# Down stage, second block: two more groups by seven, with sums of weights formed on the spot, in another order

## The chip, the cores and the metric

The kernel runs on one core of one Trainium2 chip. The metric is device time in microseconds (us). The kernel before was run three times: 1461.22, 1462.11 and 1462.31 us, median 1462.11.

## What is computed

The reference is one layer of a hybrid of attention and feed-forward over 256 tokens of width 2048, all in 32-bit floats. The change touches its last line alone, the product with `w_down`:

```python
h2 = rms_norm(x, g_ffn[l])
u = causal_depthwise_conv(h2 @ w_up[l], conv_w[l], conv_b[l])
u_gate, u_val = jnp.split(u, 2, axis=-1)
x = x + (jax.nn.silu(u_gate) * u_val) @ w_down[l]      # (256 x 5632) @ (5632 x 2048)
```

## The kernel before

**Precision.** Every 32-bit operand is split in a high part `hi` (a cast on ScalarE, ACT) and a remainder `lo` (a subtraction on VectorE, DVE). A product is three matmuls on TensorE (PE): hi by hi, lo by hi, hi by lo (function `three`, lines 326 to 330). Line 328 is the first, 329 the second, 330 the third, which is the first to read the weights' lo. `parts` (line 318) makes hi (line 322) and lo (line 323) of a piece of weights of up to 1024 columns. There are four buffers for hi and four for lo.

**Blocks and groups.** The Down stage computes its output in two blocks of 1024 columns (`nb` 0 and 1). In each, the 44 k-tiles of 128 rows are taken in 22 groups of two. A group is a 2 x 2 by 2 x 2 block product: two token tiles (t) by two k-tiles (j), times two k-tiles by two column halves (n).

- By **eight** (`eight`, line 389): the eight products, accumulated in four PSUM banks X. That is 24 matmuls, two loads of 512 KB (line 384) and two pieces to split.
- By **seven** (`seven`, line 412): Strassen's scheme in Winograd's form with seven products, 21 matmuls, accumulated in the same X and in four further banks Y. It needs four sums of weights, T1, T3, T4 and T2, and four sums of activations, FS1 to FS4. The sums of weights were formed earlier in the kernel in the background and written to DRAM (`pair_sums_ahead`, `half_sums`, `kept_for`). `seven` loads half a k-tile together with T3 into `raw0` (lines 415, 416), the other k-tile into `raw1` (384), T1 and T2 (419), and T4 (421): five DMAs and 1.75 MiB, and splits them as three pieces of 1024 columns and one of 512.
- In the gate stage the sums of weights are formed on the spot: `prepared` (line 436) loads both k-tiles a group ahead and makes the four sums by four additions on DVE (lines 440 to 443) into two buffers of their own; `seven_here` uses them.

**Sums of activations.** A "form" (`form`, line 1276, by `pair_sums`, line 332) makes FS1 to FS4 of a group on DVE (337 to 342) and splits them (344 on ACT, 346 on DVE). Eleven are made in block 0 and reused by block 1; those for groups 11 and above are written over activations that block 1's eights have read (`s_of`, line 1261). All forms share one scratch buffer, tag `ts` (`tmp_d`, line 1274), with the gathering below.

**The order.** A string gives each block's order: `e` is an eight, `s` a seven, `f` a form. The strings are `d_plans`, lines 228 to 231. Groups by seven count up from 0, eights from the number of sevens. The code is traced in that order, and Tile's scheduler makes each engine's instruction order from it; in this stage PE's order isn't pinned by the code.

**Buffers of raw weights.** Loads are counted from the start of the stage. After the first ten, the count modulo six picks the place (`raw_tile`, line 1109): four share the four buffers of tag `raw`, one has a buffer of the stage (`raw_d`, line 1291), one has `xu`. Every load of weights goes through SyncE's queue (SP), in order.

**The end.** After the last seven, `gather` (line 348) adds the Y banks to the result in eight additions on DVE (lines 355 to 365), in a chain through two scratch halves. It advances at `tick`, twice a group. In the block's very last group (`by_bank`, line 390) the products are ordered bank by bank; the last bank is cut in two, its second half called `apart`. Lines 1303 and 1307 add the X banks to the result and lines 1305 to 1310 store it through ACT's queue.

Of the kernel before, what the change touches and what calls it, by code (L numbers as in the profile page):

```python
# [12 lines left out]
ALU = mybir.AluOpType  # L13
# [4 lines left out]
NT = S // P  # L18
# [24 lines left out]
def hybrid_block(  # L43
# [25 lines left out]
    nc = tc.nc  # L69
# [12 lines left out]
    def bank(name):  # L82
        return pp.tile([P, 512], F32, tag="bank", name=name)
# [14 lines left out]
    def later(gen):  # L98
        waiting.append(gen)
# [3 lines left out]
    def tick(beside=True):  # L103
        if beside:
            for g in background:
                next(g, None)
        while waiting and len(active) < window[0]:
            active.append([waiting.popleft(), 0])
        for a in list(active):
            if a[1] > 0:  # L110
                a[1] -= 1
                continue
            try:
                a[1] = next(a[0]) or 0
            except StopIteration:
                active.remove(a)
# [7 lines left out]
    def finish():  # L124
        while waiting or active:
            tick(beside=False)
# [76 lines left out]
    def k_tiles(name):  # L203
# [23 lines left out]
    g_plans = (("", "esesesee", "esesesee"), ("esesesee", "esesesee", "esesesee"))  # L227
    d_plans = (
        "efefefef" + "sef" * 4 + "ssefsfssfssee",
        "efefef" + "sss" + "esss" * 3 + "ssee",  # L230
    )
    T1, T3, T4, T2 = range(4)
    FS2, FS4, FS3, FS1 = range(4)
    in_order = tc.keep_in_program_order
# [5 lines left out]
        (name, by_k(w), nb, pr, h)  # L240
        for name, w, plans in (("o", w_out, o_plans), ("d", w_down, d_plans))
        for nb, plan in enumerate(plans)
        for pr in range(plan.count("s"))
        for h in range(2)
    )

# [71 lines left out]
    def parts(src, name):  # L318
        n = src.shape[1]
        hi = wp.tile([P, PIECE], F32R, tag="hi", bufs=SBUFS, name=f"hi_{name}")  # L320
        lo = wp.tile([P, PIECE], F32R, tag="lo", bufs=SBUFS, name=f"lo_{name}")
        nc.scalar.copy(hi[:, :n], src)  # L322
        nc.vector.tensor_tensor(lo[:, :n], src, hi[:, :n].bitcast(F32), ALU.subtract)  # L323
        return [(hi[:, i : i + 512], lo[:, i : i + 512]) for i in range(0, n, 512)]

    def three(o, ah, al, w, first=False, last=False):
        fix = in_order if ordered[0] else lambda ins: ins
        fix(nc.tensor.matmul(o, lhsT=ah, rhs=w[0], start=first, stop=False))  # L328
        fix(nc.tensor.matmul(o, lhsT=al, rhs=w[0], start=False, stop=False))  # L329
        fix(nc.tensor.matmul(o, lhsT=ah, rhs=w[1], start=False, stop=last))  # L330
# [36 lines left out]
    def blocked(name, w, nb, n0, plan, pair, sums, raw_tile, t4_tile, gathered, ready=None, form=None, apart=None):  # L367

        wv = by_k(w)
        X = [[bank(f"x{name}{nb}_{t}_{n}") for n in range(2)] for t in range(NT)]  # L370
        Y = []
        ns = plan.count("s")

        def a_of(p, j, t):
            v = pair(p, j)
# [6 lines left out]
        def load(k):  # L382
            raw = raw_tile(f"raw_{name}{nb}_{k}")
            nc.sync.dma_start(raw, wv[:, k, n0 : n0 + PIECE])
            return raw

        go_on = lambda: tick(beside=name != "g")
# [48 lines left out]
        def prepared(p):  # L436
            raw0, raw1 = load(2 * p), load(2 * p + 1)
            t13, t42 = (t4_tile(f"t{i}_{name}{nb}_{p}") for i in range(2))
            b0, b1, u, v = (w.rearrange("p (n c) -> p n c", n=2) for w in (raw0, raw1, t13, t42))
            nc.vector.tensor_tensor(u[:, 0], b0[:, 0], b0[:, 1], ALU.add)  # L440
            nc.vector.tensor_tensor(u[:, 1], b0[:, 1], b1[:, 1], ALU.add)
            nc.vector.tensor_tensor(v[:, 1], u[:, 0], b1[:, 1], ALU.add)
            nc.vector.tensor_tensor(v[:, 0], v[:, 1], b1[:, 0], ALU.add)
            return raw0, raw1, t13, t42
# [14 lines left out]
            three(Y[1], *f_of(p, FS2), T2w, first, last)  # L459
            go_on()  # L460

        by_seven = seven_here if name == "g" else seven
        ahead = {}
        s, e = 0, ns
        for i, c in enumerate(plan):
            if c == "s":
                if s == 0:
                    if ready:
                        ready()
                    Y += [bank(f"y{name}{nb}_{j}") for j in range(4)]  # L470
                by_seven(s, s == 0, s == ns - 1)
                s += 1
                if s == ns:
                    later(gathered(n0, Y))
            elif c == "f":
                form()
            else:
                eight(e, i == 0, i == len(plan) - 1)
                e += 1
            if name == "g" and plan[i + 1 : i + 2] == "s":  # L480
                ahead[s] = prepared(s)
        finish()
        return X

# [200 lines left out]
    w = {}  # L685
# [30 lines left out]
    for k in range(KT):  # L716
# [18 lines left out]
        for _ in range(0 if k < 3 else 1 if k < 8 else 3):  # L735
            if squares:
                j, t = squares.popleft()
# [273 lines left out]
    for m in range(2):  # L1011
        gate = []
        for b, plan in enumerate(g_plans[m]):
            g, bias = [], []
# [26 lines left out]
            def ready():  # L1041
                finish()
                if "heads" not in issued:
                    issued.add("heads")
                    window[0] = 2
                    later(sigmoids(gate[0] + gate[1]))
                biases()
# [7 lines left out]
            if not plan:  # L1055
# [6 lines left out]
            X = blocked(  # L1062
                "g", w_in, f"{m}{b}", c0, plan, lambda p, j: xT(2 * p + j), lambda p, f: xs[:, p, f], raw_g, block,
                gathered, ready,
            )
# [5 lines left out]
        for n in range(2):  # L1071
            acc = gate[branches[0][3]][n]
            for i, (w, k0, nk, b) in enumerate(branches):
# [5 lines left out]
                for t in range(NT):  # L1079
                    g = gate[b][n]  # L1080
# [40 lines left out]
    for nb, plan in enumerate(o_plans):  # L1121
        X = blocked(
            "o", w_out, nb, nb * PIECE, plan, lambda p, j: mT[p][:, j], lambda p, f: ms[p][:, f], raw_o, t4_o[nb],
            lambda n0, Y: gather(n0, Y, block),
        )
# [20 lines left out]
    def a_pair(p):  # L1146
        if p < FA // 2:
            return aT[:, 2 * p : 2 * p + 2]
        if not ends:
            ends.append(ends_tile("a_ends", F32R).rearrange("p i (k c) -> p i k c", k=2))  # L1150
        return ends[0][:, p - FA // 2]
# [64 lines left out]
    for f0 in range(0, FT, 4):  # L1216
# [5 lines left out]
        for s in range(2):  # L1222
            ps = [bank(f"u{f0 + i}_{s}") for i in range(4)]
            c0 = s * D_FF + f0 * P
            for k in range(0, KT, 2):
                hi, lo = piece(upv[:, k : k + 2, c0 : c0 + 512], 2, 512, f"u{f0}_{s}_{k}")
                for j in range(2):
                    first, last = k + j == 0, k + j == KT - 1
                    for i in range(4):
                        c = slice(i * P, (i + 1) * P)  # L1230
# [20 lines left out]
        return dn[0].tile(shape, dt, tag=tag, name=name)  # L1251

    ov = out[0].rearrange("(t p) d -> p t d", p=P)
    N0, N1 = (plan.count("s") for plan in d_plans)
    sf = xt_pool.tile([P, 28, 2, P], F32R, tag="xt", name="sf")
    sf_more, sf_rest = [], []
    assert N0 == 11
    a_blocks = aT.rearrange("p k (l t q) -> p k l t q", l=2, t=NT)
    formed = [0]

    def s_of(p, f):


        if f == FS1:
            return a_blocks[:, 2 * p, :, 1]
        if p < 9:
            return sf[:, 3 * p + f]
        if p == 9:
            return sf_more[0][:, f] if f < 2 else sf_rest[2]
        if p == 10:  # L1270
            return sf[:, 27] if f == 0 else sf_rest[f - 1]
        return a_blocks[:, 2 * (p - N0 + N1) + f // 2, :, f % 2]

    tmp_d = lambda name: place([P, PIECE], F32, "ts", name)

# [17 lines left out]
    for nb, plan in enumerate(d_plans):  # L1293
        apart = [] if nb == 1 else None
        X = blocked(
            "d", w_down, nb, nb * PIECE, plan, lambda p, j: a_pair(p)[:, j], s_of, raw_d, junk,
            lambda n0, Y: gather(n0, Y, tmp_d), None, form, apart,
        )
        for t in range(NT):
            for n in range(2):  # L1300
                c = nb * PIECE + n * 512
                o = xres[:, t, c : c + 512]
                nc.vector.tensor_tensor(o, o, X[t][n], ALU.add)
                if (nb, t, n) == (1, 1, 1):
                    nc.scalar.dma_start(ov[:, t, c : c + 256], o[:, :256])
                    c, o = c + 256, o[:, 256:]
# [35 lines left out]
```

## Time and profile before

| | us |
|---|---|
| median of three runs | 1462.11 |
| the profiled execution's own time | 1461.49 |
| its span, first to last instruction | 1459.8 |
| Up stage's last matmul and Down stage's first | 1233 |
| first product of block 1 | 1345.2 |
| last matmul | 1455.8 |

The profile is of one execution. Each engine's instructions have a start and a duration; "L323" is line 323 of the kernel; PEld is the loading of a matmul's stationary operand, beside PE. Names are those of the program's tiles with numbers left out: `hi_d` and `lo_d` are split weights that were loaded from `w_down` (or half from there and half T3), `hi_t_d` split sums, `xd` and `yd` the banks X and Y, `sf` and `aT` sums of activations and activations, `fw` a form's scratch, `raw_g`, `t_g` and `xg` the gate stage's likes. `SPq` and `ACTq` are instructions that issue a DMA. In rows of single instructions the first number is the start and the second the duration; a row with "x2" holds two in a run. In rows of groups the numbers behind the bar are the busy time in us and the mean duration in ns.

### The profile page before, as it was taken

The numbers are of one execution on the slowest core, as the hardware profiler recorded it, in microseconds if no ns is written. First come the engines' busy times: TensorE is split into PE (matmuls) and PEld (weight loads), VectorE is DVE, ScalarE is ACT, GpSimd is POOL, SyncE is SP. The second block draws the span as 40 slices with busy tenths as digits, with TensorE's granted clock in tenths as the row PEclk, the third lists the DMA queues.
The fourth block names the chain that finished last, engine by engine and source line by source line (L and its number), as shares of the span: only waits on it lengthen the run. The fifth ranks groups of instructions, "written<-read, shape, count | busy, mean of one in ns | idle before, by whom it ended". The sixth has DMA issues, their size and how long they took to land.

```text
span 1459.8 us, 20547 instructions
## 1 busy us (share of the span) xinstructions
PE 1454.0 (100%) x7314; PEld 1230.1 (84%) x7314; DVE 1213.4 (83%) x1791; ACT 850.0 (58%) x1212; POOL 19.3 (1%) x48
## 2 busy tenths in 40 slices
PE   9999999999999999999999999999999999999998
PEld 7888888888888888888888888888888888888887
DVE  5778777776898899997887888888888877999878
ACT  6755454564564555545666556556556565676665
POOL 0000000010000000000000000000000000000000
PEclk9999999999999999999999999999999999999999
DMA  9697798777668576788877888888888866899995
GB/s 312 202 330 248 267 341 288 238 241 222 209 207 269 172 231 198 270 265 263 276 196 232 288 266 306 278 273 299 283 281 298 267 200 202 253 291 333 299 324 222
DMA packets 162534, 381.08 MB, mean 261 GB/s; under 512 B 12234, under 2 KB 27486, under 8 KB 158334
## 3 DMA queue, kind: packets, MB, share of 16 engines
q1 hardware_dynamic: 161022, 377.52, 78.9%
q10 hardware_dynamic: 1328, 2.11, 0.4%
q8 instruction: 57, 0.93, 0.3%
q14 instruction: 47, 0.39, 0.1%
q0 software_dynamic: 80, 0.13, 0.0%
HBM read 343.01 MB, written 36.70 MB: 260 GB/s over the span
## 4 chain that ended last, share of the span: by engine, by line
PE 97%; DVE 1%; DMA 1%; issue 0%; SPq 0%; ACT 0%; DVEq 0%; ACTq 0%
PE u L1231 22%; PE u L1232 11%; PE xd L329 3%; PE xd L330 3%; PE xd L328 3%; PE xg L330 3%; PE xg L329 3%; PE xg L328 3%; PE s L328 2%; PE s L330 2%; PE f L330 2%; PE f L328 2%; PE f L329 2%; PE s L329 2%; PE b L330 2%; PE b L328 2%
## 5 line engine op out<-in xcount | busy, mean ns | idle before, releaser
L1231 PE MATMUL u<-hT,hi_u 128*128 128x512 f32 x1232 | 428.3, 394 | 0.0
L1232 PE MATMUL u<-hT,lo_u 128*128 128x256 f32 x1232 | 341.3, 277 | 0.0
L1231 PEld LDWEIGHTS u<-hT,hi_u 128*128 128x128 f32 x1232 | 231.0, 188 | 53.8
L143 DVE TENSOR_TENSOR lo_u<-raw_u,hi_u 128x1024 fp32r<-128x1024 f32 x176 | 215.1, 1222 | 73.2 <-ACT hi_u L142 71.9
L142 ACT CAST hi_u<-raw_u 128x1024 fp32r<-128x1024 f32 x176 | 184.7, 1050 | 135.0 <-PE u L1231 106.7
L1232 PEld LDWEIGHTS u<-hT,lo_u 128*128 128x128 f32 x1232 | 231.2, 188 | 0.0
L323 DVE TENSOR_TENSOR lo_d<-raw_d,hi_d 128x1024 fp32r<-128x1024 f32 x88 | 106.7, 1222 | 16.2 <-ACT hi_d L322 13.8
L322 ACT CAST hi_d<-raw_d 128x1024 fp32r<-128x1024 f32 x88 | 91.7, 1053 | 38.8 <-PE xd L329 17.8
L322 ACT CAST hi_g<-raw_g 128x1024 fp32r<-128x1024 f32 (+1 forms) x80 | 77.1, 972 | 48.9 <-PE xg L329 19.2
L323 DVE TENSOR_TENSOR lo_g<-raw_g,hi_g 128x1024 fp32r<-128x1024 f32 (+1 forms) x80 | 88.6, 1119 | 4.1 <-ACT hi_g L322 4.1
L142 ACT CAST hi_f<-raw_f 128x1024 fp32r<-128x1024 f32 (+1 forms) x40 | 38.5, 967 | 51.8 <-PE f L329 42.8
L330 PE MATMUL xg<-lo_g,xT 128*128 128x512 f32 x175 | 68.1, 389 | 0.0
L329 PE MATMUL xg<-hi_g,xT 128*128 128x512 f32 x175 | 68.1, 389 | 0.0
L328 PE MATMUL xg<-hi_g,xT 128*128 128x512 f32 x175 | 68.1, 389 | 0.0
L143 DVE TENSOR_TENSOR lo_f<-raw_f,hi_f 128x1024 fp32r<-128x1024 f32 (+1 forms) x40 | 44.6, 1118 | 22.3 <-ACT hi_f L142 21.7
L143 DVE TENSOR_TENSOR lo_s<-raw_s,hi_s 128x1024 fp32r<-128x1024 f32 (+1 forms) x40 | 44.7, 1117 | 20.9 <-ACT hi_s L142 20.9
L1231 PE MATMUL u<-hT_rest,hi_u 128*128 128x512 f32 x176 | 62.0, 394 | 0.0
L142 ACT CAST hi_b<-raw_b 128x1024 fp32r<-128x1024 f32 x32 | 33.6, 1051 | 45.2 <-DMA raw_b<-in_w_br_fox_dram 15.8
L142 ACT CAST hi_s<-raw_s 128x1024 fp32r<-128x1024 f32 (+1 forms) x40 | 38.4, 961 | 36.8 <-PE s L329 23.9
L1182 ACT ACTIVATE y<-u,taps 128x256 f32<-128x256 f32 x88 | 49.6, 596 | 16.3 <-DVE u L1177 16.2
L330 PE MATMUL xd<-lo_d,aT 128*128 128x512 f32 x148 | 57.6, 389 | 0.0
L328 PE MATMUL xd<-hi_d,aT 128*128 128x512 f32 x148 | 57.6, 389 | 0.0
(520 smaller groups left out, 3473.1 us busy)
## 6 DMA issues: line engine op xcount, KB each, us to landing
raw_u<-in_w_up_dram SPq DMA_DIRECT2D x176, 512.0 KB, 4.5
raw_g<-in_w_in_dram SPq DMA_DIRECT2D x96, 512.0 KB, 4.4
raw_d<-in_w_down_dram SPq DMA_DIRECT2D x63, 512.0 KB, 5.4
pre_d<-in_w_down_dram SPq DMA_DIRECT2D x17, 1024.0 KB, 6.2
kept_d<-pre_d SPq DMA_DIRECT2D x17, 1024.0 KB, 6.2
raw_f<-in_w_in_dram SPq DMA_DIRECT2D x32, 512.0 KB, 4.9
raw_s<-in_w_in_dram SPq DMA_DIRECT2D x32, 512.0 KB, 5.2
raw_t_d<-kept_d SPq DMA_DIRECT2D x25, 512.0 KB, 5.8
```

The costliest lines, as they stand in the source:

```text
L142: pin(nc.scalar.copy(hi[:, :m], raw[:, :m]))
L143: pin(nc.vector.tensor_tensor(lo[:, :m], raw[:, :m], hi[:, :m].bitcast(F32), ALU.subtract))
L322: nc.scalar.copy(hi[:, :n], src)
L323: nc.vector.tensor_tensor(lo[:, :n], src, hi[:, :n].bitcast(F32), ALU.subtract)
L328: fix(nc.tensor.matmul(o, lhsT=ah, rhs=w[0], start=first, stop=False))
L329: fix(nc.tensor.matmul(o, lhsT=al, rhs=w[0], start=False, stop=False))
L330: fix(nc.tensor.matmul(o, lhsT=ah, rhs=w[1], start=False, stop=last))
L1182: nc.scalar.activation(y, u[:, 2:], AF.Identity, scale=tap(2), bias=tap(3))
L1231: nc.tensor.matmul(ps[i], lhsT=hi[:, j, c], rhs=hT(k + j), start=first, stop=False)
L1232: nc.tensor.matmul(ps[i][:, :S], lhsT=lo[:, j, c], rhs=hT(k + j)[:, :S], start=False, stop=last)
```

## The change

The second block's plan becomes `efss` four times, then `issefssisse`. Sixteen groups go by seven and six by eight, in place of fourteen and eight; five forms in place of three. `i` is a new kind of group by seven. Its weight sums are formed on the spot: `begun`, traced right behind the group ahead, loads both k-tiles and makes T1, T3 and T2 by three additions, T1 and T3 into a scratch buffer of tag `ts`, T2 over half of the first k-tile's own buffer. `seven_over` splits the other half, forms T4 over it, and goes on as `seven_here` does. The groups that have their sums in DRAM are still fourteen in this block, with other numbers.

```diff
     d_plans = (
         "efefefef" + "sef" * 4 + "ssefsfssfssee",
-        "efefef" + "sss" + "esss" * 3 + "ssee",
+        "efss" * 4 + "issefssisse",
     )
+    sevens = lambda plan: [c for c in plan if c in "si"]
...
-        for pr in range(plan.count("s"))
+        for pr, c in enumerate(sevens(plan))
+        if c == "s"
...
+        def begun(p):
+            raw0, raw1, t13 = load(2 * p), load(2 * p + 1), tmp_d(f"t_{name}{nb}_{2 * p}")
+            b0, b1, u = (w.rearrange("p (n c) -> p n c", n=2) for w in (raw0, raw1, t13))
+            nc.vector.tensor_tensor(u[:, 0], b0[:, 0], b0[:, 1], ALU.add)
+            nc.vector.tensor_tensor(u[:, 1], b0[:, 1], b1[:, 1], ALU.add)
+            nc.vector.tensor_tensor(b0[:, 1], u[:, 0], b1[:, 1], ALU.add)
+            return raw0, raw1, t13
+
+        def seven_over(p, first, last):
+            raw0, raw1, t13 = ahead.pop(p)
+            (B00,) = parts(raw0[:, :512], f"{name}{nb}_{2 * p}")
+            three(Y[0], *a_of(p, 0, 0), B00, first, last)
+            nc.vector.tensor_tensor(raw0[:, :512], raw0[:, 512:], raw1[:, :512], ALU.add)
+            B10, B11 = parts(raw1, f"{name}{nb}_{2 * p + 1}")
+            three(X[0][0], *a_of(p, 1, 0), B10)
+            three(X[0][1], *f_of(p, FS4), B11)
+            go_on()
+            T1w, T3w = parts(t13, f"t_{name}{nb}_{2 * p}")
+            three(Y[2], *f_of(p, FS1), T1w, first, last)
+            three(Y[3], *f_of(p, FS3), T3w, first, last)
+            T4w, T2w = parts(raw0, f"t_{name}{nb}_{2 * p + 1}")
+            three(X[1][0], *a_of(p, 1, 1), T4w)
+            three(Y[1], *f_of(p, FS2), T2w, first, last)
+            go_on()
...
+            elif plan[i + 1 : i + 2] == "i":
+                ahead[s] = begun(s)
...
-        return a_blocks[:, 2 * (p - N0 + N1) + f // 2, :, f % 2]
+        over = a_pair(p - N0 + N1).rearrange("p k (l t q) -> p k l t q", l=2, t=NT)
+        return over[:, f // 2, :, f % 2]
```

The rest of the diff replaces counts of `s` by counts of `s` and `i`, and picks the function by the letter.

More of the change, by code (lines that the diff above doesn't have):

```diff
@@ L371, in blocked @@
         Y = []
-        ns = plan.count("s")
+        ns = len(sevens(plan))
         def a_of(p, j, t):
@@ L460, in seven_here @@
             go_on()
-        by_seven = seven_here if name == "g" else seven
+        def begun(p):
[21 more added lines that the diff above has]
+            go_on()
+        by_seven = {"s": seven_here if name == "g" else seven, "i": seven_over}
         ahead = {}
@@ L465, in blocked @@
         for i, c in enumerate(plan):
-            if c == "s":
+            if c in "si":
                 if s == 0:
@@ L470, in blocked @@
                     Y += [bank(f"y{name}{nb}_{j}") for j in range(4)]
-                by_seven(s, s == 0, s == ns - 1)
+                by_seven[c](s, s == 0, s == ns - 1)
                 s += 1
@@ L1253, in hybrid_block @@
     ov = out[0].rearrange("(t p) d -> p t d", p=P)
-    N0, N1 = (plan.count("s") for plan in d_plans)
+    N0, N1 = (len(sevens(plan)) for plan in d_plans)
     sf = xt_pool.tile([P, 28, 2, P], F32R, tag="xt", name="sf")
```

## The prediction

> **What bounds the kernel now.** I read the totals first, then the Down stage by engine, then single instructions there.
>
> ```profile
> span 1459.8 us, 20547 instructions
> PE 1454.0 (100%) x7314; PEld 1230.1 (84%) x7314; DVE 1213.4 (83%) x1791; ACT 850.0 (58%) x1212; POOL 19.3 (1%) x48
> ```
>
> PE is busy for the whole span, but ends of matmuls are modelled, so the second block (from 1345.2 us to its last matmul) has to be read from distances between starts:
>
> ```profile
> 1345.20:1455.80 110.60, 110.60 (x494) 91.66 (x492) 92.49 (x109) 68.45 (x82) 0.00 (x0) 1.00 0.84 287
> 1375.80:1395.50 19.70, 19.70 (x88) 16.31 (x87) 15.27 (x15) 13.14 (x15) 0.00 (x0) 1.00 0.95 332
> ...
> 1366.49 0.39 PE L328 MATMUL yd<-hi_d,aT 128*128 128x512 f32 x1
> 1366.94 0.39 PE L330 MATMUL yd<-lo_d,aT 128*128 128x512 f32 x1
> 1371.25 0.39 PE L328 MATMUL yd<-hi_d,aT 128*128 128x512 f32 x1
> ```
>
> In the windows the columns after the length are PE, PEld, DVE, ACT, POOL, clock, DMA share, GB/s. A group by seven has 21 matmuls: 1371.25 - 1366.49 = 4.76 us, or 0.2267 us each. An eight has 24, 5.44 us. One eight and three sevens are 87 matmuls, 19.72 us, the length of the second window. The block's 486 products would take 110.2 us, and its window is 110.6. PE waits for nothing here at full clock, so the matmul count sets the block's length.
>
> How much the others may slip, the casts and subtractions tell (ACT, then DVE; the number before "<-" in brackets is idle time):
>
> ```profile
> 1363.10 1.05 ACT L322 CAST hi_d<-raw_d 128x1024 fp32r<-128x1024 f32 x1 [0.74 <-PE yd L329]
> 1367.82 1.06 ACT L322 CAST hi_d<-raw_d 128x1024 fp32r<-128x1024 f32 x1 [0.47 <-PE yd L329]
> 1364.19 2.59 DVE L323 TENSOR_TENSOR lo_d<-raw_d,hi_d 128x1024 fp32r<-128x1024 f32 x2 [1.10 <-ACT hi_d L322]
> 1366.87 1.83 DVE L323 TENSOR_TENSOR lo_t_d<-raw_t_d,hi_t_d 128x1024 fp32r<-128x1024 f32 x2
> 1368.91 2.58 DVE L323 TENSOR_TENSOR lo_d<-raw_d,hi_d 128x1024 fp32r<-128x1024 f32 x2 [0.21 <-ACT hi_d L322]
> 1347.10 1.21 DVE L323 TENSOR_TENSOR lo_d<-raw_d,hi_d 128x1024 fp32r<-128x1024 f32 x1
> 1348.23 0.41 DVE L340 TENSOR_TENSOR fw<-fw 128x256 f32<-128x256 f32 x1
> ```
>
> Casts are released by PE, which frees one of four hi buffers. The first lo of the group at 1366.49 ends at 1364.19 + 1.23 = 1365.42 and is first read at 1366.94. So the lead is 1.5 us, however early the weights come. A 1024-wide subtraction occupies DVE for 1348.23 - 1347.10 = 1.13 us when the next operation doesn't depend on it, though its record is 1.22 long.
>
> **The change, part by part.** *Matmuls.* Two eights become groups by seven: 6 fewer, 6 x 0.2267 = -1.36 us. That is all there is to gain.
>
> *DMAs.* Counting issues, block two had 8 x 2 + 14 x 5 = 86, and has 6 x 2 + 14 x 5 + 2 x 2 = 86. Bytes: 8 x 1 + 14 x 1.75 = 32.5 MiB, and 6 + 24.5 + 2 = 32.5 again. The densest pattern gets lighter: one eight and three sevens moved 332 GB/s without a PE gap; one eight and two sevens are 4.5 MiB in 14.96 us, or 315 GB/s. I cost the transfers at nothing, hidden behind PE; without that cover, see the third rival.
>
> *Activation sums.* Two forms more. Their DVE and ACT work, of which three lay in the window already:
>
> ```profile
> L337 DVE TENSOR_TENSOR fw<-aT 128x512 f32<-128x512 f32 x3 | 2.1, 687 | 0.0
> L340 DVE TENSOR_TENSOR fw<-fw 128x256 f32<-128x256 f32 x3 | 1.2, 417 | 0.0
> L341 DVE SCALAR_TENSOR_TENSOR fw<-fw 128x128 f32<-128x128 f32 x3 | 0.9, 292 | 0.1
> L342 DVE TENSOR_TENSOR fw<-fw 128x128 f32<-128x128 f32 x3 | 0.9, 288 | 0.0
> L344 ACT CAST aT<-fw 128x128 fp32r<-128x128 f32 x12 | 3.1, 296 | 1.3 <-DVE fw L342 0.7 <-DVE fw L340 0.5
> L346 DVE TENSOR_TENSOR aT<-fw,aT 128x128 fp32r<-128x128 f32 x12 | 2.7, 286 | 0.0
> ```
>
> One form is 0.69 + 0.42 + 0.29 + 0.29 + 4 x 0.29 = 2.8 us of DVE by durations, some 2.2 by distances (each 0.08 less where nothing depends). A stretch "efss" then needs 2 x 1.13 + 2.2 + 2 x (3 x 1.13 + 0.61) = 12.5 us of DVE in 14.96 of PE. It fits: nothing on the path. Their writes overlay activations that the eight just ahead reads, as before; three such stood without a gap.
>
> *The two groups with sums formed on the spot.* Each adds four 512-wide additions, at 0.61 (an independent one) to 0.72 us (a dependent one, below): 2.45 us at the lower price. Against an eight, it also has 1.5 pieces more to split. DVE then needs 4.0 + 2.45 = 6.4 us in a group of 4.76. Three additions are issued ahead, in the preceding seven's slot: 4.0 + 1.83 = 5.83 against 4.76, 1.07 late; the fourth stays in its own, 4.61 against 4.76. The lead is thinner here too: the new group's first piece has only 3 matmuls, so its second and third piece have 12 matmuls of cover instead of 15, that is 0.68 us less, 1.5 - 0.7 = 0.8. So 1.07 - 0.8, about 0.3 us of PE stall per group, if the weights have landed. Next late are casts and lo of the following seven, which recovers 0.76 a group. Whether they have landed, only the gate stage's like groups show (waits of its first addition, one such row, and the only PE gap among its 15):
>
> ```profile
>   DMA raw_g<-in_w_in_dram: 11.5, 9
> 378.44 0.69 DVE L440 TENSOR_TENSOR t_g<-raw_g 128x512 f32<-128x512 f32 x1 [2.25 <-DMA raw_g<-in_w_in_dram]
> 421.76 0.39 PE L329 MATMUL xg<-hi_t_g,xT 128*128 128x512 f32 x1
> 422.28 0.50 PE L330 MATMUL xg<-lo_t_g,xT 128*128 128x512 f32 x1
> ```
>
> There DVE stood still 11.5 / 9 = 1.3 us in 9 of 15, and everything behind it in its queue with it (lo for PE), yet PE lost just 0.3 us once: an eight ahead gave long cover. Here a seven is ahead. Bounds per group: 0 (additions spread into idle gaps) and 1.3 + 1.83 - 0.76 (idle in a seven's slot) - 0.8 = 1.6. I take 0.5, nearer to the gate stage, 1.0 in both.
>
> *The end.* The plan ended in two eights after the last seven, now in one. The result's gathering (eight additions) had two eights of 5.44 us to hide in:
>
> ```profile
> 1442.68 2.35 DVE L323 TENSOR_TENSOR lo_d<-raw_d,hi_d 128x1024 fp32r<-128x1024 f32 x2
> 1444.95 0.68 DVE L356 TENSOR_TENSOR e<-e,yd 128x512 f32<-128x512 f32 x1
> 1444.72 0.39 PE L328 MATMUL xd<-hi_d,a_ends 128*128 128x512 f32 x1
> 1448.54 0.69 DVE L359 TENSOR_TENSOR xres_again<-xres_again,e 128x512 f32<-128x512 f32 x1
> 1449.26 0.69 DVE L361 TENSOR_TENSOR e<-e,yd 128x512 f32<-128x512 f32 x1
> 1344.10 2.47 DVE L1303 TENSOR_TENSOR xres_again<-xres_again,xd 128x512 f32<-128x512 f32 x4
> 1450.16 0.39 PE L328 MATMUL xd<-hi_d,a_ends 128*128 128x512 f32 x1
> 1455.55 0.28 PE L330 MATMUL apart<-lo_d,a_ends 128*128 128x256 f32 x1
> 1455.95 0.42 DVE L1307 TENSOR_TENSOR xres_again<-xres_again,apart 128x256 f32<-128x256 f32 x1
> 1456.40 0.34 ACTq L1308 DMA_DIRECT2D out_dram<-xres_again  x1
> ```
>
> Let T be the start of the eight that follows the last seven, 1444.72 here. DVE is through with that eight's lo at T + 0.2 and takes the second addition (L356). Seven dependent ones at 1449.26 - 1448.54 = 0.72 end at T + 5.3. Then four last additions (2.47 together) and L1307, 0.42: T + 8.2. Before, the last store was issued at 1456.40 - 1450.16 = 6.2 after its last eight began. So the end comes 2.0 us later; if the additions fill each other's gaps (11 x 0.61 + 0.42 + 0.2 = 7.3) 1.1. I take 1.8, nearer to the chained rows, since the order in the code is chain first.
>
> **Sum.** -1.36 + 1.0 + 1.8 = +1.4 us on the span of 1459.8. The profiled execution took 1461.49 with what lies around the span, 0.6 under the shown runs' median of 1462.11; the same difference on the median gives **1463.5**.
>
> **The rivals.** *Full gain* (0.15): no stall, and the gathering disappears beside the last eight: 1462.1 - 1.4 = 1460.7. For it, a window of the first block:
>
> ```profile
> 1280.00:1295.00 15.00, 15.00 (x68) 12.43 (x67) 14.96 (x24) 10.33 (x14) 0.00 (x0) 1.00 0.90 285
> ```
>
> DVE was 14.96 of 15 us busy, and PE started its matmuls (x68) without a gap. Against it: the end's arithmetic above.
>
> *Slower by a stalled DVE queue* (0.27): the new groups' first additions stand in DVE's queue before their weights are there. Place: the two seven-to-new boundaries; price 1.6 us each. -1.36 + 3.2 + 1.8 = +3.6, 1465.7, with a worse wait (2.25, the row) up to 1467.6. It decides from 1.25 us of stall a group on. For it: 9 waits of 15 in the gate stage. Against: six raw buffers here.
>
> *A raw buffer held long* (0.08): the first weight buffer is now read until the group's last split, some 3.9 us after the group starts, where the plain seven frees it ahead of its start. The load that reuses it is the second next group's second, and for the first new group it has no other buffer (the 88th load of the stage falls on a buffer with one place).
>
> ```profile
> raw_d<-in_w_down_dram SPq DMA_DIRECT2D x21, 512.0 KB, 6.1
> ```
>
> 3.9 + 6.1 = 10.0; its lo is read at 9.52 + 1.36 + 0.45 = 11.3, so its cast must start 2.4 earlier (1.06 + 1.23 and 0.1 between), at 8.9. SP's queue waits behind it, too. Price 1.1 us: 1464.6. Against it: with the queue empty a load should land sooner.
>
> *DVE operations never overlap* (0.05): every operation would cost its whole duration. A seven's slot with three additions is 4.36 + 2.07 = 6.43, late by 1.67, and 0.29 more in the next; 2.0 - 0.8 = 1.2 stall each. -1.36 + 2.4 + 1.8 = +2.8, 1464.9. The distance of 1.13 against 1.22 speaks against it. The Trainium skill, "VectorE: DVE Perf Modes", section "The DRAIN you can't avoid", says that the next operation doesn't start until the pipe is empty; by that rule this rival holds, and the row has starts 0.08 us sooner than that.
>
> *The change doesn't do what it says* (0.02): the plan strings count 14 + 2 + 6 = 22 groups, so hardly; 1462.1.
>
> **How the numbers follow.** The forecast (0.43) spans 1462.0 to 1464.9. The range 1460.7 to 1467.0 reaches from the full gain to the slow rival's bad end. Within 0.2% (2.9 us, about what a measurement can tell from no change) means 1459.2 to 1465.0: forecast, full gain, buffer and whole-duration cases mostly, 0.70. Slower: 0.27 and the upper tail of others, 0.28. Faster by 0.2% needs twice the saved matmuls: 0.02.
>
> **What would show it.** Right: 480 products in the block at 0.2267 us; gaps of a few tenths at the second or third piece of the two new groups; L1308 issued about 8 us after the last eight starts. The rivals: a DVE wait for raw weights at the new additions with PE gaps over 1.2 us; an ACT wait for a load two groups after the first new one. I would be wrong if PE gaps appeared in "efss", or if the last store came 6.2 us after the last eight's start.

## The result, and the profile after

| | before | after |
|---|---|---|
| median of six runs, us | 1461.86 | 1466.48 |
| lowest and highest, us | 1461.22, 1462.75 | 1465.48, 1467.49 |
| profiled execution, us | 1461.49 | 1467.49 |
| its span, us | 1459.8 | 1465.8 |

The ratio is 1.0031 (95% interval 1.0018 to 1.0044): the changed kernel is slower by 4.6 us. It lies inside the range, but three us above the number that was forecast.

**Where the time lies.** The totals and the second block of the changed kernel, in the columns of the prediction's first two fences:

```profile
span 1465.8 us, 20589 instructions
PE 1456.3 (99%) x7308; PEld 1230.4 (84%) x7308; DVE 1223.3 (83%) x1819; ACT 854.8 (58%) x1224; POOL 19.3 (1%) x48
...
1346.30:1459.70 113.40, 111.00 (x488) 90.06 (x486) 100.87 (x135) 73.43 (x94) 0.00 (x0) 1.00 0.82 279
```

The saving is there: six matmuls fewer (7308 for 7314), at full clock. But the window has grown by 2.8 us to 113.40, and PE, which filled its window to the last hundredth before, is short of it by 2.4. To place the loss, the block is cut at starts of matmuls. First the block's first product before (at 1345.41, not at 1345.2 as the table of times before has it; the start of its last eight, 1450.16, is in the prediction), then rows of after:

```profile
1345.41 0.39 PE L328 MATMUL xd<-hi_d,aT 128*128 128x512 f32 x1
```

```profile
1346.55 0.39 PE L330 MATMUL xd<-hi_d,aT 128*128 128x512 f32 x1
...
1401.63 0.39 PE L330 MATMUL yd<-hi_d,aT 128*128 128x512 f32 x1
...
1454.24 0.39 PE L330 MATMUL xd<-hi_d,a_ends 128*128 128x512 f32 x1
```

- *Before the block:* 1346.55 against 1345.41, 1.1 us. The change touches nothing there. In twelve profiles of kernels that differ only in this block, its first product came between 1345.1 and 1347.3 us. That is a difference between executions, and a reason to take sizes from inside the block.
- *"efss" four times, without the last seven:* that seven starts at 1401.63, and 1401.63 - 1346.55 = 55.08 us for 243 matmuls, 0.2267 each. No stall up to there.
- *Up to the last eight:* before 1450.16 - 1345.41 = 104.75 for 462 matmuls (104.72 at 0.2267). After 1454.24 - 1346.55 = 107.69 for 456 (103.36). The stall is **4.3 us**, all of it behind 1401.63.
- *From the last eight to the last store:* 6.24 before, 8.56 after, **+2.3 us** (rows below). From that store to the end of the span it is 3.4 before and 3.0 after.

The sum, -1.36 + 4.3 + 2.3 - 0.4 = +4.8 us, fits the 4.6 of the medians.

**The stall.** PE's timeline in the changed kernel, at four of the six places where a start is late (the other two are alike to the third pair, 0.24 us each, at 1440.6 and 1442.3):

```profile
1401.86 0.39 PE L331 MATMUL yd<-hi_d,aT 128*128 128x512 f32 x1
1403.01 0.50 PE L332 MATMUL yd<-lo_d,aT 128*128 128x512 f32 x1 [0.76 <-DVE lo_d L325]
1403.35 0.40 PE L330 MATMUL yd<-hi_d,sf 128*128 128x512 f32 x1
...
1408.39 0.39 PE L331 MATMUL xd<-hi_d,aT 128*128 128x512 f32 x1
1408.95 0.50 PE L332 MATMUL xd<-lo_d,aT 128*128 128x512 f32 x1 [0.16 <-DVE lo_d L325]
...
1419.10 0.40 PE L331 MATMUL xd<-hi_d,aT 128*128 128x512 f32 x1
1419.79 0.50 PE L332 MATMUL xd<-lo_d,aT 128*128 128x512 f32 x1 [0.29 <-DVE lo_d L325]
...
1433.33 0.39 PE L331 MATMUL yd<-hi_d,aT 128*128 128x512 f32 x1
1434.76 0.50 PE L332 MATMUL yd<-lo_d,aT 128*128 128x512 f32 x1 [1.04 <-DVE lo_d L325]
```

Each late start is that of a third matmul, the first reader of the weights' lo, and each waits for DVE. What a pair loses is the distance less 0.23: 0.92, 0.33, 0.46, 1.20, and 0.24 twice, 3.4 in all. The matmul behind each is late once more, by 0.11 (1403.35 - 1403.01 = 0.34): 0.7. The rest is in smaller ones. By groups, from the start of one to the start of the next, the 4.3 us are: 1.10 in the seven ahead of the first new group, 0.48 in that new group, 0.66 in the second seven behind it, 1.34 in the seven ahead of the second new group and 0.75 in that one.

The two large ones are in the sevens *ahead* of the new groups. DVE there (and ACT's cast, between):

```profile
1399.94 0.69 DVE L467 TENSOR_TENSOR t_d<-raw_d 128x512 f32<-128x512 f32 x1 [1.74 <-DMA raw_d<-in_w_down_dram]
1401.12 0.69 DVE L468 TENSOR_TENSOR t_d<-raw_d,raw_d 128x512 f32<-128x512 f32 x1 [0.49 <-DMA raw_d<-in_w_down_dram]
1401.73 2.35 DVE L325 TENSOR_TENSOR lo_d<-raw_d,hi_d 128x1024 fp32r<-128x1024 f32 x2
...
1432.88 0.69 DVE L467 TENSOR_TENSOR t_d<-raw_d 128x512 f32<-128x512 f32 x1 [3.22 <-DMA raw_d<-in_w_down_dram]
1433.49 2.35 DVE L325 TENSOR_TENSOR lo_d<-raw_d,hi_d 128x1024 fp32r<-128x1024 f32 x2
```

```profile
1429.68 1.05 ACT L324 CAST hi_d<-raw_d 128x1024 fp32r<-128x1024 f32 x1 [0.74 <-DVE lo_t_d L325]
```

```profile
1393.07 1.47 SPq L386 DMA_DIRECT2D raw_d<-in_w_down_dram  x2
...
1425.51 1.47 SPq L386 DMA_DIRECT2D raw_d<-in_w_down_dram  x2
```

The additions are traced behind the seven ahead, yet in DVE's queue the first two of them (at the second new group the first alone) stand ahead of its subtractions. The new groups' weights were asked for at 1393.07 and 1425.51 and were there 6.9 and 7.4 us later. DVE stood still for them, 1.74 + 0.49 and 3.22 us. For the second, the seven's hi was ready at 1429.68 + 1.05 = 1430.73, but its lo began at 1433.49, and PE stopped for it at 1433.6. This is the rival of the stalled DVE queue, at the places it named.

The pairs at 1408, 1440 and 1442 lie inside the new groups, at their second and third piece: the backlog that the sum had. The pair at 1419 is two groups after the first new one, and it is the rival of the held buffer. ACT and SP there:

```profile
1417.42 1.05 ACT L324 CAST hi_d<-raw_d 128x1024 fp32r<-128x1024 f32 x1 [2.31 <-PE xd L331]
```

```profile
1411.19 2.60 SPq L386 DMA_DIRECT2D raw_d<-in_w_down_dram  x3
```

The load that reuses the new group's first buffer could be issued only when that group's last split had been through (1411.19), and its cast followed 6.2 us later. ACT's wait is put down to PE, but in one experiment below (`shifted`) the same cast is released by PE at 1414.95, and in another (`pinned`) it waits for the DMA.

**The end**, DVE and the last store:

```profile
1453.86 1.23 DVE L325 TENSOR_TENSOR lo_d<-raw_d,hi_d 128x1024 fp32r<-128x1024 f32 x1
1455.01 0.68 DVE L358 TENSOR_TENSOR e<-e,yd 128x512 f32<-128x512 f32 x1
...
1456.33 0.68 DVE L1333 TENSOR_TENSOR xres_again<-xres_again,xd 128x512 f32<-128x512 f32 x1
...
1460.77 0.68 DVE L367 TENSOR_TENSOR xres_again<-xres_again,e 128x512 f32<-128x512 f32 x1
1461.55 0.69 DVE L1333 TENSOR_TENSOR xres_again<-xres_again,xd 128x512 f32<-128x512 f32 x1
1462.35 0.42 DVE L1337 TENSOR_TENSOR xres_again<-xres_again,apart 128x256 f32<-128x256 f32 x1
```

```profile
1462.80 0.34 ACTq L1338 DMA_DIRECT2D out_dram<-xres_again  x1
```

Last additions (L1333) stand between those of the gathering (L358 to L367), but fill only a part of its gaps: eleven starts from 1455.01 to 1461.55 are 0.65 us apart in the mean, between the 0.61 of an independent and the 0.72 of a dependent addition. They begin 0.77 us after the eight (1454.24), not 0.2, and the last two steps depend on each other (0.78 and 0.80 apart). The last store goes out 8.56 after the eight began.

### The profile page after: what moved, and what is told of

Its sections match the earlier page's. It is cut to its first block, busy times and chain, and to the rows that moved or that the text cites. A ratio compares the mean times of both kernels' runs of the same rounds, so it can differ in the third digit from the quotient of the medians.

```text
span 1465.8 us, 20589 instructions
## 1 busy us (share of the span) xinstructions
PE 1456.3 (99%) x7308; PEld 1230.4 (84%) x7308; DVE 1223.3 (83%) x1819; ACT 854.8 (58%) x1224; POOL 19.3 (1%) x48
## 4 chain that ended last, share of the span: by engine, by line
PE 97%; DVE 1%; DMA 1%; ACT 0%; issue 0%; DVEq 0%; SPq 0%
PE u L1260 22%; PE u L1261 11%; PE xg L330 4%; PE xg L332 4%; PE xg L331 4%; PE xd L332 3%; PE xd L330 3%; PE xd L331 3%; PE s L330 2%; PE s L332 2%; PE f L332 2%; PE f L331 2%; PE f L330 2%; PE s L331 2%; PE b L330 2%; PE b L332 2%
## 5 line engine op out<-in xcount | busy, mean ns | idle before, releaser
L324 ACT CAST hi_d<-raw_d 128x1024 fp32r<-128x1024 f32 (+1 forms) x88 | 90.7, 1043 | 42.2 <-PE xd L331 13.5
L325 DVE TENSOR_TENSOR lo_d<-raw_d,hi_d 128x1024 fp32r<-128x1024 f32 (+1 forms) x88 | 104.9, 1207 | 10.6 <-ACT hi_d L324 9.6
L324 ACT CAST hi_t_g<-t_g 128x1024 fp32r<-128x1024 f32 x30 | 31.5, 1051 | 40.8 <-PE xg L331 35.8
L330 PE MATMUL s<-hi_s,xT 128*128 128x512 f32 (+1 forms) x140 | 54.1, 386 | 0.0
```

## The experiments

Two theories stood at first. *Queue:* most of the stall is the first additions' wait for weights at the head of DVE's queue. *Work:* DVE has too much to do around the new groups, wherever its additions stand. Beside them: the end (one eight instead of two), the held buffer, and the new order by itself. "Stall" below is the distance from the block's first product to its last eight, less 0.2267 us a matmul; "end" is the distance from the last eight's start to the last store's issue. Both are read from one profiled execution of each kernel. The ratios to the kernel before are those on record; they can differ by up to 0.0006 from the quotient of the medians. Diffs are against the changed kernel unless they say otherwise. The kernel before had medians of 1461.63, 1461.96 and 1461.88 us in the three sets of runs.

### The additions held in the order of the code (pinned)

```diff
-            nc.vector.tensor_tensor(u[:, 0], b0[:, 0], b0[:, 1], ALU.add)
-            nc.vector.tensor_tensor(u[:, 1], b0[:, 1], b1[:, 1], ALU.add)
-            nc.vector.tensor_tensor(b0[:, 1], u[:, 0], b1[:, 1], ALU.add)
+            in_order(nc.vector.tensor_tensor(u[:, 0], b0[:, 0], b0[:, 1], ALU.add))
+            in_order(nc.vector.tensor_tensor(u[:, 1], b0[:, 1], b1[:, 1], ALU.add))
+            in_order(nc.vector.tensor_tensor(b0[:, 1], u[:, 0], b1[:, 1], ALU.add))
```

> The changed kernel, but the three additions of a group with sums formed on the spot are kept in program order on DVE, that is behind the splits of the seven ahead. Queue theory (the additions stand at the head of DVE's queue before their weights have landed, and the lo's behind them make PE wait; 2.3 of the 4.1 us of PE gaps): the two gaps at the sevens ahead of the new groups vanish, DVE waits for raw weights under 0.3 us, time near 1464.3. Work theory (DVE simply has too much to do around the new groups): the gaps only move, time stays near 1466.5.

Measured: 1464.13 us, 1.0013 of before (1.0004 to 1.0021), 2.35 below the changed kernel's median. The stall is 1.3 us instead of 4.3. DVE, then PE, at the first new group:

```profile
1401.31 1.83 DVE L325 TENSOR_TENSOR lo_t_d<-raw_t_d,hi_t_d 128x1024 fp32r<-128x1024 f32 x2
1403.05 0.69 DVE L467 TENSOR_TENSOR t_d<-raw_d 128x512 f32<-128x512 f32 x1
1403.65 0.69 DVE L468 TENSOR_TENSOR t_d<-raw_d,raw_d 128x512 f32<-128x512 f32 x1
```

```profile
1401.15 0.39 PE L331 MATMUL yd<-hi_d,aT 128*128 128x512 f32 x1
1401.38 0.39 PE L332 MATMUL yd<-lo_d,aT 128*128 128x512 f32 x1
```

The same additions now follow the seven's four subtractions and wait for nothing (no bracket), and the pair that lost 0.92 us is at the bare 0.23. The amount of work is the same, so the queue theory holds for 3 of the 4.3 us. It also shows that the weights were not late: the additions were early. By groups, the two sevens ahead of the new groups lose nothing now, and the new groups 0.33 us each, with their weights there: that is the backlog of 0.3 that the prediction worked out for this case.

The rest of the 1.3 is 0.08 in an eight and 0.50 in the second seven behind the first new group, with the one clear pair (PE, then ACT):

```profile
1417.16 0.40 PE L331 MATMUL xd<-hi_d,aT 128*128 128x512 f32 x1
1417.72 0.50 PE L332 MATMUL xd<-lo_d,aT 128*128 128x512 f32 x1 [0.17 <-DVE lo_d L325]
```

```profile
1415.36 1.05 ACT L324 CAST hi_d<-raw_d 128x1024 fp32r<-128x1024 f32 x1 [2.18 <-DMA raw_d<-in_w_down_dram]
```

Here the cast's wait carries the name of the load: the held buffer.

### The first two additions from data that is there (resident)

```diff
-            nc.vector.tensor_tensor(u[:, 0], b0[:, 0], b0[:, 1], ALU.add)
-            nc.vector.tensor_tensor(u[:, 1], b0[:, 1], b1[:, 1], ALU.add)
+            nc.vector.tensor_tensor(u[:, 0], xres[:, 0, :512], xres[:, 0, 512:1024], ALU.add)
+            nc.vector.tensor_tensor(u[:, 1], xres[:, 1, :512], xres[:, 1, 512:1024], ALU.add)
```

T1 and T3 of the two groups, and T2 with T1, are then no sums of weights.

> The changed kernel, but the first two additions read columns of the result that lie in SBUF since long, in place of the loaded weights (so T1 and T3 are not the weights' sums). Same DVE work, no wait for a load at them. Queue theory: the DVE waits of 5.5 us go, PE gaps fall from 4.1 to below 2 us, time near 1464.3. Work theory: PE gaps and time as in the changed kernel, 1466.5.

Measured: 1464.27 us, 1.0016 (1.0007 to 1.0024); stall 0.8 us. The additions are as many and as long, only two of them need no load: again the work isn't the loss. The new groups themselves lose 0.05 us in all. Two waits remained, 1.95 and 0.49 us, both at the third addition, which does read weights. The first stood ahead of the seven's subtractions, and that seven lost 0.65 us:

```profile
1399.73 0.69 DVE L469 TENSOR_TENSOR raw_d<-t_d,raw_d 128x512 f32<-128x512 f32 x1 [1.95 <-DMA raw_d<-in_w_down_dram]
```

The second stood behind the first subtractions of the seven ahead of it and cost nothing. So the position in the queue, whichever addition holds it, is what costs. (The median isn't below that of `pinned`, though the stall is 0.5 us less: the medians don't tell differences of that size.)

### One eight at the end, in the kernel before (tail)

Against the kernel before:

```diff
-        "efefef" + "sss" + "esss" * 3 + "ssee",
+        "efefefe" + "sss" + "esss" * 3 + "sse",
```

> The kernel before, with one eight moved from the end of the second block's plan to its beginning, so that one eight follows the last seven instead of two; nothing else. End theory (the gathering and the last additions no longer fit beside one eight): last store issued about 8.3 us after the last eight starts instead of 6.2, time 1.9 us over before, near 1463.8. Rival (the gathering stays hidden, the late end of the changed kernel comes from its stalls): time as before, 1461.9.

Measured: 1464.0 us, 1.0010 (1.0001 to 1.0019); stall 0.03. PE's last eight, DVE, and ACT's queue:

```profile
1450.42 0.39 PE L328 MATMUL xd<-hi_d,a_ends 128*128 128x512 f32 x1
```

```profile
1450.77 0.68 DVE L356 TENSOR_TENSOR e<-e,yd 128x512 f32<-128x512 f32 x1
...
1457.32 0.69 DVE L1303 TENSOR_TENSOR xres_again<-xres_again,xd 128x512 f32<-128x512 f32 x1
```

```profile
1458.56 0.34 ACTq L1308 DMA_DIRECT2D out_dram<-xres_again  x1
```

The store comes 8.14 us after the eight begins, 1.9 later than with two eights, though only the place of one eight has changed. The additions start 0.35 after it, and the eleven up to 1457.32 are (1457.32 - 1450.77) / 10 = 0.65 apart in the mean. The changed kernel has 0.42 us more, since its DVE reaches the gathering 0.42 later (0.77).

### The first buffer on another place (shifted)

```diff
+        loads[0] += 4 * nb
```

At the start of block 1 the count of loads moves on by four, so that the new groups' first load falls on one of the four buffers of tag `raw`.

> The changed kernel, but the count that places raw weights is moved on by four at the second block, so that both new groups' first weights fall on the four shared buffers, of which any free one can be taken. Buffer theory (the load two groups after the first new group waits for the one buffer that is held to that group's end; 0.6 us of PE gap): no load is issued late there and the gap about 17 us after the first stall is gone. Rival: the gap stays, as it comes from DVE's backlog or from the form.

One execution: 1464.98 us, stall 1.9 us. SP and ACT at the place of the third pair:

```profile
1408.47 0.33 SPq L386 DMA_DIRECT2D raw_d<-in_w_down_dram  x1
```

```profile
1414.95 1.06 ACT L324 CAST hi_d<-raw_d 128x1024 fp32r<-128x1024 f32 x1 [0.30 <-PE xd L331]
```

The load is out 2.7 us sooner (2.3 when both are taken from the new group's start), the cast is released by PE again, and the pair is gone: that seven loses 0.03 us instead of 0.66. This agrees with the held buffer as the cause of the pair's 0.46 + 0.11 us, though it is one execution and the edit moves the later loads to other places too.

At the second new group the first addition again waited ahead of a seven's subtractions, but that seven lost nothing (DVE, then PE):

```profile
1430.16 0.69 DVE L467 TENSOR_TENSOR t_d<-raw_d 128x512 f32<-128x512 f32 x1 [1.59 <-DMA raw_d<-in_w_down_dram]
```

```profile
1432.01 0.39 PE L330 MATMUL yd<-hi_d,aT 128*128 128x512 f32 x1
...
1432.47 0.39 PE L332 MATMUL yd<-lo_d,aT 128*128 128x512 f32 x1
```

The addition starts 1.85 us before the seven here; in the changed kernel it was 0.23 (1432.88 and 1433.11). The rest of the difference to the changed kernel isn't this edit's alone: the first additions waited 3.1 us for their loads in this execution, and 5.0 in the changed kernel's. How long that wait is changes with where loads stand, and perhaps from execution to execution; these runs don't separate the two.

### The new order with the old groups (order)

Against the kernel before, fourteen sevens, eight eights and three forms, in turn:

```diff
-        "efefef" + "sss" + "esss" * 3 + "ssee",
+        "efss" * 3 + "esss" * 2 + "essee",
```

> The kernel before with its fourteen sevens, eight eights and three forms of the second block in turn (efss three times, esss twice, essee), the end as before. Theory: the new alternation costs nothing by itself, 0 us of stall, time as before, 1461.6. Rival: sevens and forms that come earlier in the block crowd DMA or DVE there and part of the changed kernel's loss is the order's: over 1462.5.

Measured: 1462.45 us, 1.0004 (0.9995 to 1.0013). Stall 0.03, end 6.24, as before:

```profile
1347.10:1457.60 110.50, 110.50 (x494) 91.67 (x492) 92.03 (x109) 68.65 (x82) 0.00 (x0) 1.00 0.83 287
```

PE fills the window. The order and the forms' places cost nothing by themselves.

### An eight ahead of each new group (behind_e)

```diff
-        "efss" * 4 + "issefssisse",
+        "efsss" + "efss" + "eifsss" + "efsss" + "eifssse",
...
+        loads[0] += 4 * nb
```

> The changed kernel with its two new groups put right behind an eight (efsss efss eifsss efsss eifsss e), as in the gate stage, and their first weights on the four shared buffers; the end is still one eight. Queue theory: an eight ahead gives long cover, so the same waits cost PE under 0.5 us; only the late end is left: -1.4 + 1.9 + 0.3, 1462.5. Work theory (DVE has more to do than it can, wherever the groups stand): stalls of 2 us and more, over 1464.

Measured: 1463.16 us, 1.0010 (1.0001 to 1.0018). The stall is down to 0.1 us, though the first additions still waited for weights, 1.1 us in all. The run changes two things at once, though: an eight is ahead, and the additions start 4.0 and 1.9 us before these eights, far earlier than the 0.5 and 0.2 us before the sevens of the changed kernel. It doesn't show that it was the eight that helped. And the end took 9.05 us: three sevens stand right ahead of the only eight left, PE lost some 0.4 us inside it, and the gathering began 1.26 us after the eight, 0.49 later than in the changed kernel, which is the whole of the 9.05 - 8.56. The saving was spent there.

### Two eights at the end (two_e)

```diff
-        "efss" * 4 + "issefssisse",
+        "efsss" + "efsss" + "eifsss" + "eifsss" + "fssee",
...
+        if p == 15:
+            return sf[:, f]
```

(The second edit gives the sixteenth group's sums of activations a place whose reader is through.)

> Sixteen sevens, the new groups right behind an eight, and two eights at the end again (efsss efsss eifsss eifsss fssee); the fifth form writes over the first group's sums, which the block has used by then, instead of an eight's activations. If stall and late end are the whole loss, the six matmuls saved are left: 1461.6 - 1.4 + 0.2 = 1460.4. If there is another cost of sixteen sevens, it stays at 1461.6 or above.

Measured: 1461.54 us, 0.9999 (0.9990 to 1.0007); end 6.24 again; stall 1.4 us. DVE, then PE, at the first new group:

```profile
1409.17 0.69 DVE L467 TENSOR_TENSOR t_d<-raw_d 128x512 f32<-128x512 f32 x1 [1.66 <-DMA raw_d<-in_w_down_dram]
```

```profile
1411.06 0.50 PE L332 MATMUL xd<-lo_d,aT 128*128 128x512 f32 x1 [0.38 <-DVE lo_d L325]
```

An eight is ahead here too, yet a wait of 1.66 us ahead of its lo reached PE, and the eight lost 0.67 us. Most of the rest of the 1.4, 0.18 and 0.52 us, is in the sevens right behind the two new groups. With the end repaired, 1.4 of stall eats the 1.36 us saved.

### The additions on GpSimd (pool)

```diff
-            nc.vector.tensor_tensor(u[:, 0], b0[:, 0], b0[:, 1], ALU.add)
-            nc.vector.tensor_tensor(u[:, 1], b0[:, 1], b1[:, 1], ALU.add)
-            nc.vector.tensor_tensor(b0[:, 1], u[:, 0], b1[:, 1], ALU.add)
+            nc.gpsimd.tensor_tensor(u[:, 0], b0[:, 0], b0[:, 1], ALU.add)
+            nc.gpsimd.tensor_tensor(u[:, 1], b0[:, 1], b1[:, 1], ALU.add)
+            nc.gpsimd.tensor_tensor(b0[:, 1], u[:, 0], b1[:, 1], ALU.add)
...
-            nc.vector.tensor_tensor(raw0[:, :512], raw0[:, 512:], raw1[:, :512], ALU.add)
+            nc.gpsimd.tensor_tensor(raw0[:, :512], raw0[:, 512:], raw1[:, :512], ALU.add)
```

> The changed kernel with the new groups' four additions on GpSimd instead of DVE. Queue theory: waiting for weights there holds up no lo; left are the held buffer (0.6) and the end (1.9): 1461.6 - 1.4 + 2.5 = 1462.7, if an addition there takes under 1.5 us. Rival: GpSimd's additions are so slow (over 2 us) that casts of T1 and T3 come late: stalls as in the changed kernel or worse, 1466 and above.

Measured: 1467.01 us, 1.0034 (1.0022 to 1.0046); stall 4.4 us. GpSimd's timeline, ACT's waits (us in total, times, longest) and DVE's timeline:

```profile
1401.26 2.27 POOL L468 TENSOR_TENSOR t_d<-raw_d,raw_d 128x512 f32<-128x512 f32 x1
...
1407.06 2.14 POOL L476 TENSOR_TENSOR raw_d<-raw_d,raw_d 128x512 f32<-128x512 f32 x1 [1.30 <-DVE lo_d L325]
```

```profile
ACT hi_t_d L324 <- POOL raw_d L476: 5.5, 2, 3.1
```

```profile
1402.31 4.01 DVE L325 TENSOR_TENSOR lo_t_d<-raw_t_d,hi_t_d 128x1024 fp32r<-128x1024 f32 x2
...
1407.98 2.31 DVE L325 TENSOR_TENSOR lo_t_d<-t_d,hi_t_d 128x1024 fp32r<-128x1024 f32 x1
```

DVE's queue waits for no load now, and still nothing is gained: an addition takes 1.6 to 2.3 us there, T4's stands right on the path to its cast, and DVE's subtractions beside them stretch (4.01 us for the pair that took 1.83 in the first experiment). One loss took another's place.

### New groups directly behind eights, two sevens between (spread, spread_pinned)

```diff
-        "efss" * 4 + "issefssisse",
+        "efsss" + "eissfs" + "efsss" + "eissfs" + "fssee",
...
+        if p == 15:
+            return sf[:, f]
```

`spread_pinned` holds the additions in the order of the code as well.

> As two_e, but plain and new groups alternate and the forms stand behind the new groups' followers (efsss eissfs efsss eissfs fssee). The first addition still may stand in DVE's queue ahead of the eight's lo's. Theory: the form's chain of small operations no longer falls between a new group's lo's; stall from 1.4 to about 0.8; time near 1461.3. Rival: the stall comes from the wait alone and stays at 1.4, 1461.7.

> As spread, with the three early additions kept in program order on DVE, behind the eight's lo's. Queue theory: no DVE wait for weights reaches PE, stall under 0.3 us, last store 6.5 us after the last eight starts; time 1.0 to 1.4 under before, near 1460.7. Rival: something else of sixteen sevens costs over 1 us, time 1461.5 or more.

Measured: 1461.76 us, 1.0001 (0.9992 to 1.0010), stall 0.5; and 1461.88, 0.9998 (0.9989 to 1.0007), stall 0.5. Both ends are 6.24. In `spread` the one wait, 1.32 us ahead of an eight's subtractions, cost that eight 0.34. In `spread_pinned` no addition waits and the new groups lose 0.03 us in all; 0.43 is lost in a seven near the block's end, whose first lo stands behind five operations of a form; some 7 us earlier a cast had waited 1.50 us for its load. Which of the two is the cause wasn't tested. In the profiles the blocks are 0.8 and 0.9 us shorter than before up to the last eight (1.36 saved, 0.5 lost), but the medians don't show it. The expectation of `spread_pinned`, a stall under 0.3 us and a time near 1460.7, was missed, and its time is that of its rival. Executions of one kernel differ by 2 us and more, part of it from the start of the kernel. So nothing that was tried beats the kernel before; the changed kernel's whole loss is recovered, and its saving stays below what these runs can tell.

**When a wait reaches PE.** Taken together, the profiles say more than each alone. The table has the cases in which an addition that waited for weights stood ahead of the first subtraction for the group ahead: the start of the last such addition, the start of that group on PE, the distance between them, and what the group's first late start lost.

| run and new group | wait, us | group ahead | addition starts | group starts | distance | lost |
|---|---|---|---|---|---|---|
| changed kernel, second | 3.22 | seven | 1432.88 | 1433.11 | 0.23 | 1.20 |
| changed kernel, first | 1.74 + 0.49 | seven | 1401.12 | 1401.63 | 0.51 | 0.92 |
| `shifted`, first | 1.54 + 0.49 | seven | 1400.67 | 1401.38 | 0.71 | 0.71 |
| `two_e`, second | 1.66 | eight | 1409.17 | 1410.07 | 0.90 | 0.54 |
| `resident`, first | 1.95 | seven | 1399.73 | 1400.64 | 0.91 | 0.51 |
| `spread`, first | 1.32 | eight | 1363.72 | 1364.95 | 1.23 | 0.20 |
| `shifted`, second | 1.59 | seven | 1430.16 | 1432.01 | 1.85 | 0 |
| `behind_e`, second | 0.62 | eight | 1422.10 | 1424.03 | 1.93 | 0 |
| `two_e`, first | 0.59 | eight | 1383.45 | 1385.41 | 1.96 | 0 |
| `behind_e`, first | 0.51 | eight | 1375.79 | 1379.79 | 4.00 | 0 |

Wherever something is lost, distance and loss add up to 1.42 to 1.44 us, behind sevens and eights alike. It can be worked out from rows: 0.61 from the addition to the subtraction behind it, 1.23 for that subtraction and 0.05 to its reader on PE, less the 0.45 from the group's start to its third matmul, 1.44. So neither the length of the wait nor an eight or a seven ahead decides, but how long before the group's start the weights are there.

## Why the prediction was right in part

- *The matmuls* were right: 480 products in the block, and 0.2267 us wherever nothing stalls.
- *DMAs, forms and order at nothing* were right away from the new groups: 243 matmuls of "efss" without a stall in the changed kernel, and no stall in the experiment on the order. The prediction named PE gaps in "efss" as a sign that it would be wrong, and the two largest gaps do lie in the last seven of an "efss"; the new group behind put them there, not the pattern.
- *The end* was right in kind and near in size. 1.8 was taken, 2.0 worked out, and 2.3 measured (1.9 by itself). From the first of these additions to the end of the last it takes 7.8 us, near the chained reading's 7.9 and above the lower bound's 7.1. The reason given, that the order in the code is chain first, was wrong: the two kinds of additions alternate, and the row comes out near the chain's length only since several steps still depend on the one ahead, the last two above all. So the near size is in part luck. The start was the mis-sized term, 0.77 for 0.2: a backlog of subtractions, after groups with little slack, delays the gathering too.
- *"I take 0.5, nearer to the gate stage"* is the step that failed. Both groups were to cost 1.0 us; with the sevens ahead of them they cost 3.7, and the held buffer another 0.66. The backlog of 0.3 for weights that have landed was right (0.33 each in `pinned`). The wait was not: it was sized by the gate stage's mean, 1.3 us, where the waits were 2.2 and 3.2, so that even the upper bound, 1.6 a group, was too low. And the mechanism was off: the gate stage was said to be spared by the eight ahead. The table shows losses behind an eight and none behind a seven. What spared the gate stage's row in the prediction fits the same rule: its addition starts at 378.44, 2.9 us before its eight (381.38). The prediction had no term for how early the weights come before the group ahead.
- *The stalled queue* (0.27, 1465.7) was the right mechanism at the right places and near in time to 1466.5; its 3.2 us of stall fit the 3.0 that `pinned` gave back. Its counter-argument, "six raw buffers here", didn't hold: buffers decide when a load may be issued, while the addition's place decides who waits. It didn't ask whether the additions would stand ahead of the seven's subtractions, and that decided: held behind them, they found their weights. Why the scheduler put them ahead was not tried.
- *The held buffer* (0.08) is real: the load, the place and the 6.1 us of landing as worked out, the price 0.57 us instead of 1.1, since PE was late itself by then (0.48 us in the new group). In `resident` that load was cast 5.7 us after its issue, and the seven lost 0.14 us in all.
- *Whole durations for DVE* fell. L467 at 1432.88 and the subtraction behind it at 1433.49 are 0.61 apart at a record of 0.69. The prediction set the Trainium skill's "VectorE: DVE Perf Modes", section "The DRAIN you can't avoid", against the rows; the first paragraph of that section ends by saying that a next operation which isn't held starts earlier, and sends the reader on to "Two Vector instructions with no wait between them". The traces agree with that end of it.
- *The full gain* (0.15) was left far behind; its window of a busy DVE said nothing of an addition that waits.
- *The range* was said to reach to the slow rival's bad end, but stops at 1467.0 where that rival was worked out up to 1467.6. At a median of 1466.48 it made no difference.

## What to carry to other kernels

An operation that reads a fresh load costs whoever stands behind it in an in-order queue, not its own reader: ask first where the scheduler will put it, and hold it behind the work whose inputs are there. Waits measured in one stage can't be carried to another: read instead how long before the group ahead starts the load lands, and compare that with the work that must follow it (1.43 us here). And where work is removed from the last block, count what gathering the result still has to hide in: one eight less at the end cost more than six saved matmuls.

## What the runs showed of the hardware

- GpSimd slows DVE while it works. A 1024-wide subtraction beside a GpSimd addition took 2.31 us, and 1.22 alone. The Trainium skill, "GPSIMD Engine Reference", section "1. Specifications", says that GpSimd's way to SBUF is shared with VectorE and is contended by VectorE instructions with two SBUF inputs; the subtraction has two, and the trace agrees. Spans on GpSimd itself are rough in these profiles; the two durations are DVE's.
- A matmul that starts late after a wait for DVE is followed by the next one late as well: 0.34 us to the next start instead of 0.23 (1403.01 to 1403.35).
- The same code before block 1 took from 1345.1 to 1347.3 us in twelve executions, so a difference of one us between two profiles' ends means nothing until the stage has been measured from its own first matmul.
